# Moving gamma's load from ScalarE's queue to SyncE's, between and behind the halves of the first tile

## The chip, the cores and the metric

One core of a Trainium2 chip. The metric is the time of one execution on the device in microseconds (us). Before the change it was 239.57 us, the median of 3 runs (239.4 to 239.84). Smaller is better; a change within 2% either way counts as the same. All runs told here are fast runs with a granted clock of 1.000.

## The reference

```python
# x: (8, 512, 2048) float32, gamma: (2048,) float32; result (8, 1024, 2048) float32
x_rep = np.repeat(x, 2, axis=1)
rms = np.sqrt((x_rep ** 2).mean(axis=-1, keepdims=True) + 1e-6)
return (x_rep / rms * gamma[None, None, :]).astype(np.float32)
```

Every row of x is normalised, multiplied by gamma and written twice. Read once and written once that is 33.6 MB in and 67.1 MB out.

## The kernel before

The 4096 rows are eight tiles of 512 rows (128 partitions, four rows each). A tile has a buffer of 64 KB a partition, of which there are three. Loads fill the second half of a buffer; results fill it from the front, and the store writes the whole buffer out.

```python
def load(i, eng, parts=1):
    y = rows.tile([P, K * R, D], f32, name="y")      # K = 4, R = 2, D = 2048
    step = K // parts
    for k in range(0, K, step):
        at = K * (R - 1) + k
        eng.dma_start(out=y[:, at : at + step, :], in_=x_t[i, :, k : k + step, :])
    ys.append(y)
# ... square: Square with a sum and Sqrt on ScalarE; scale: reciprocal and
# scalar_tensor_tensor (x * rstd * gamma) on VectorE; repeat: copies on ScalarE and VectorE ...
ctx.enter_context(tc.manual_schedule())
load(0, nc.sync, parts=2)
gamma_b = singles.tile([P, D], f32, name="gamma_b")
cuts = [0, *range(D // 4, D + 1, D // 8)]            # one piece of 512 elements, six of 256
for c0, c1 in zip(cuts, cuts[1:]):
    nc.scalar.dma_start(out=gamma_b[0:1, c0:c1], in_=gamma[c0:c1].partition_broadcast(1))
nc.gpsimd.partition_broadcast(out_ap=gamma_b[:], in_ap=gamma_b[0:1, :])
eps_t = singles.tile([P, 1], f32, name="eps_t")
nc.vector.memset(eps_t, eps)
load(1, nc.sync)
load(2, nc.sync)
loads_after = {2: (3, 4, 5), 4: (6, 7)}
for i in range(ntiles):                              # 8
    compute(i)                                       # 4 x (square, scale), then repeat
    store(i, 0, K)
    for j in loads_after.get(i, ()):
        load(j, nc.sync)
```

## Time and profile before

| | before |
|---|---|
| median of 3 runs | 239.57 us |
| span of the profiled run | 237.9 us |
| packets of SyncE's queue (q1), share of sixteen DMA engines' time | 98.5% |
| ScalarE, VectorE busy | 42%, 41% |

What the change touches is the way gamma comes in, and two rows of the list of costliest groups show it. The columns are line, engine, operation, output and inputs, shapes, count; then busy time and mean ns of one; then the idle time of the engine just before them and what ended most of it.

```profile
L74 DVE SCALAR_TENSOR_TENSOR y<-y,rstd,gamma_b 128x2048 f32<-128x2048 f32 x32 | 75.3, 2352 | 4.1 <-POOL gamma_b L96 3.0
...
L96 POOL PARTITION_BROADCAST gamma_b<-gamma_b x1 | 2.3, 2294 | 12.2 <-DMA y<-in_x_dram 12.2
```

VectorE waits 3.0 us for the broadcast, and the broadcast waits 12.2 us. The name behind the arrow, a load of x, is a trap: the broadcast needs no part of x. The eight completion semaphores are shared in turn, one of gamma's pieces and the second half of tile 0 count on the same one, and the profile names whichever it finds there. That it was gamma is told by the chain of waits, which the prediction quotes.

### The profile page before, as it was taken

The numbers are of one execution on the slowest core, as the hardware profiler recorded it, in microseconds if no ns is written. First come the engines' busy times: TensorE is split into PE (matmuls) and PEld (weight loads), VectorE is DVE, ScalarE is ACT, GpSimd is POOL, SyncE is SP. The second block draws the span as 40 slices with busy tenths as digits, with TensorE's granted clock in tenths as the row PEclk, the third lists the DMA queues.
The fourth block names the chain that finished last, engine by engine and source line by source line (L and its number), as shares of the span: only waits on it lengthen the run. The fifth ranks groups of instructions, "written<-read, shape, count | busy, mean of one in ns | idle before, by whom it ended". The sixth has DMA issues, their size and how long they took to land.

```text
span 237.9 us, 287 instructions
## 1 busy us (share of the span) xinstructions
DVE 96.5 (41%) x73; ACT 101.0 (42%) x106; POOL 2.5 (1%) x5
## 2 busy tenths in 40 slices
DVE  0049999960000000059999960000199990000000
ACT  2697999900000000099999920000599960000000
POOL 0030000000000000000000000000000000000000
DMA  7999998989899998999998999989998989999994
GB/s 265 436 446 441 441 441 353 530 353 496 386 452 430 397 485 353 441 441 441 441 518 364 464 419 430 452 369 430 435 518 364 518 364 485 397 452 430 408 474 176
DMA packets 2464, 100.69 MB, mean 423 GB/s; under 512 B 279, under 2 KB 285, under 8 KB 286
## 3 DMA queue, kind: packets, MB, share of 16 engines
q1 hardware_dynamic: 2448, 100.66, 98.5%
q14 instruction: 2, 0.02, 0.0%
q10 hardware_dynamic: 14, 0.01, 0.0%
HBM read 33.56 MB, written 67.11 MB: 423 GB/s over the span
## 4 chain that ended last, share of the span: by engine, by line
DMA 58%; ACT 12%; DVE 9%; issue 1%; POOLq 1%; ACTq 1%; SPq 0%
DMA y<-in_x_dram 33%; DMA out_dram<-y 21%; ACT sq L64 8%; DVE y L74 7%; DMA gamma_b<-in_gamma_dram 4%; ACT y L81 3%; DVE y L81 2%; ACT rms L68 1%; POOLq L136 1%; ACTq L95 1%; DVE rstd L73 0%; POOLq L96 0%; SPq L56 0%
## 5 line engine op out<-in xcount | busy, mean ns | idle before, releaser
L64 ACT ACTIVATE sq<-y 128x2048 f32<-128x2048 f32 x32 | 59.7, 1865 | 87.8 <-DMA y<-in_x_dram 87.8
L74 DVE SCALAR_TENSOR_TENSOR y<-y,rstd,gamma_b 128x2048 f32<-128x2048 f32 x32 | 75.3, 2352 | 4.1 <-POOL gamma_b L96 3.0
L73 DVE RECIPROCAL rstd<-rms 128x1 f32<-128x1 f32 x32 | 5.0, 158 | 94.6 <-ACT rms L68 94.3
L81 ACT COPY y<-y 128x4096 f32<-128x4096 f32 x8 | 28.7, 3590 | 1.4 <-DVE y L74 1.4
L81 DVE COPY y<-y 128x4096 f32<-128x4096 f32 x8 | 18.3, 2294 | 0.3
L68 ACT ACTIVATE rms<-ss,eps_t 128x1 f32<-128x1 f32 x32 | 9.4, 295 | 1.0
L64 ACT ACTIVATION_READ_ACCUMULATOR sq<-y 128x1 f32 x32 | 6.0, 187 | 0.0
L64 ACT ACT_TABLE_LOAD x1 | 1.3, 1283 | 3.0 <-issue 3.0
L96 POOL PARTITION_BROADCAST gamma_b<-gamma_b x1 | 2.3, 2294 | 12.2 <-DMA y<-in_x_dram 12.2
L68 ACT ACT_TABLE_LOAD x1 | 1.3, 1283 | 0.0
L98 DVE MEMSET eps_t<- 128x1 f32 x1 | 0.1, 59 | 0.8 <-PEq L125 0.8
L125 POOL MEMSET const-uint8-127<- 128x1 uint8 x1 | 0.1, 102 | 0.0
L125 POOL MEMSET const-bfloat16-1.0<- 128x1 bf16 x1 | 0.1, 101 | 0.0
L125 POOL MEMSET const-float32-0.0<- 128x1 f32 x1 | 0.1, 98 | 0.2 <-issue 0.2
L125 POOL MEMSET const-float32-1.0<- 128x1 f32 x1 | 0.1, 98 | 0.0
## 6 DMA issues: line engine op xcount, KB each, us to landing
y<-in_x_dram SPq DMA_DIRECT2D x7, 4096.0 KB, 14.6
y<-in_x_dram SPq DMA_DIRECT2D x2, 2048.0 KB, 7.4
out_dram<-y SPq DMA_DIRECT2D x8, 24.4
gamma_b<-in_gamma_dram ACTq DMA_DIRECT2D x6, 1.0 KB
gamma_b<-in_gamma_dram ACTq DMA_DIRECT2D x1, 2.0 KB
```

Of the source, the lines that this page charges most:

```text
L64: nc.scalar.activation(out=sq[:], in_=ys[i][:, K * (R - 1) + k, :], func=Act.Square, accum_out=ss[:])
L68: nc.scalar.activation(out=rms[:], in_=ss[:], func=Act.Sqrt, scale=inv_d, bias=eps_t[:])
L73: nc.vector.reciprocal(out=rstd[:], in_=rms[:])
L74: nc.vector.scalar_tensor_tensor(out=ys[i][:, R * k, :], in0=ys[i][:, K * (R - 1) + k, :], scalar=rstd[:], in1=gamma_b[:], op0=Alu.mult, o ...
L81: copy(out=y_r[:, k0:k1, 1, :], in_=y_r[:, k0:k1, 0, :])
L95: nc.scalar.dma_start(out=gamma_b[0:1, c0:c1], in_=gamma[c0:c1].partition_broadcast(1))
L96: nc.gpsimd.partition_broadcast(out_ap=gamma_b[:], in_ap=gamma_b[0:1, :])
L98: nc.vector.memset(eps_t, eps)
L125: nc = _bacc.Bacc("TRN2", target_bir_lowering=False, num_devices=1)
L136: with _tile.TileContext(nc) as tc:
```

## The change

Its intent can be read from its order: gamma no longer takes turns with the loads from a second queue, but goes on the loads' own queue, six pieces right behind the first half of tile 0 and one behind the second half. ScalarE no longer issues DMAs.

```diff
-    load(0, nc.sync, parts=2)
     gamma_b = singles.tile([P, D], f32, name="gamma_b")
     cuts = [0, *range(D // 4, D + 1, D // 8)]
-    for c0, c1 in zip(cuts, cuts[1:]):
-        nc.scalar.dma_start(out=gamma_b[0:1, c0:c1], in_=gamma[c0:c1].partition_broadcast(1))
+
+    def gamma_piece(c0, c1):
+        nc.sync.dma_start(out=gamma_b[0:1, c0:c1], in_=gamma[c0:c1].partition_broadcast(1))
+
+    y0 = rows.tile([P, K * R, D], f32, name="y")
+    ys.append(y0)
+    load_half(y0, 0)                     # rows 0 and 1 of the tile, on SyncE
+    for c0, c1 in zip(cuts[:-2], cuts[1:-1]):
+        gamma_piece(c0, c1)
+    load_half(y0, 1)                     # rows 2 and 3
+    gamma_piece(cuts[-2], cuts[-1])
     nc.gpsimd.partition_broadcast(out_ap=gamma_b[:], in_ap=gamma_b[0:1, :])
```

The rest of the diff only splits the helper `load` into `load_half` and `load` and drops its engine argument.

## The prediction

> **What bounds the kernel now.** I read the engine totals first, then the slices, then the queues.
>
> ```profile
> DVE 96.5 (41%) x73; ACT 101.0 (42%) x106; POOL 2.5 (1%) x5
> ...
> DMA  7999998989899998999998999989998989999994
> ...
> q1 hardware_dynamic: 2448, 100.66, 98.5%
> q14 instruction: 2, 0.02, 0.0%
> q10 hardware_dynamic: 14, 0.01, 0.0%
> HBM read 33.56 MB, written 67.11 MB: 423 GB/s over the span
> ```
>
> VectorE and ScalarE work two fifths of a span of 237.9 us; the DMA engines are at 8 or 9 tenths in every slice but the first and the last. The queue table says what they do: q1 is the queue of SyncE, with all loads and stores, and its packets alone fill 98.5% of what sixteen engines could do in the span. q10 is ScalarE's queue, with fourteen packets: seven pieces of gamma, each a data packet and a 4-byte packet that counts the semaphore. So the time is a start before the first packet (1.6 us), 100.7 MB at full rate, and an end. 100.66 MB over the 235.2 us from the first q1 packet (at 1.73) to the last (236.77, both from the packet records of the trace) is 428 GB/s; nothing in the kernel can make that shorter except fewer bytes, and nothing makes it longer unless the queue runs dry. The whole question is therefore whether the change leaves the queue dry anywhere, or takes such a gap away.
>
> The place to look is the start, where the change is. The chain of waits tells how gamma sits there, and the timeline the consequences:
>
> ```profile
> 0.72 0.51 ACTq L95
> ...
> 2.69 9.71 DMA gamma_b<-in_gamma_dram
> ...
> 12.55 2.35 POOLq L136
> 14.90 0.02 issue
> 14.92 2.35 DVE y L74
> ...
> 24.69 2.30 DVE y L81
> ...
> 27.05 25.77 DMA out_dram<-y
> 52.84 48.32 DMA y<-in_x_dram
> ```
>
> ScalarE issues seven pieces; the last, issued at 2.69, lands 9.71 us later at 12.40. Then GpSimd spreads the row over the partitions (2.3 us), VectorE runs its first multiplication at 14.92 and is busy without a break until 26.99, and the store of tile 0 is issued at 27.05. The chain names gamma at its beginning, which makes it look as if earlier gamma were earlier everything. It is not so, and the next step shows why: the store takes 25.77 us to land, far more than its own 8.39 MB need (19.6 us at 428 GB/s), because it stands in the queue behind loads. The counting packets of the load of tile 2 come at 32.41 to 33.00 in the packet records: until then the DMA engines have loads to do, whatever VectorE does. From an issue to its first packet pass about 1.0 us (0.72 to 1.73 for the first load), so the store of tile 0 could be issued as late as about 31.4 without a gap. It is issued at 27.05: **4.3 us of slack**.
>
> SyncE's own waits show a coupling that the diff does not:
>
> ```profile
> SPq L52 <- DMA y<-in_x_dram: 5.7, 1, 5.7
> ...
> SPq L52 <- DMA gamma_b<-in_gamma_dram: 0.9, 1, 0.9
> ```
>
> The DMAs take eight completion semaphores in turn. The second half of tile 0 now shares the one of gamma's first piece and waits 0.9 us for it (issue at 2.03); the load of tile 1 shares that of the first half and waits 5.7 us (issue at 8.11).
>
> **What the Trainium skill says.** On "DMA: Bandwidth & Descriptors", section "Queues, rings and completion order": SyncE and ScalarE each own one row of rings on the same sixteen engines, an engine takes turns between rows at packet boundaries, and inside a ring descriptors are consumed in order. The trace agrees: the last four gamma pieces land at 8.57, 9.85, 11.12 and 12.40, 1.27 us apart, which is two 16 KB packets of the load (0.61 us each in the packet records) plus two tiny ones. Each of gamma's packets waited its turn behind one 16 KB packet. Section "Why a DMA increments its semaphore by 16 and not by 1" of the same page: a copy that can't be split runs on one engine, and the sequencer adds the rest of the count at once. The trace agrees: each gamma semaphore has one update 0.3 to 0.6 us after the issue and one more at landing, where a load has sixteen. Section "Issuing engines are not separate DMA queues": starting DMAs from several engines saves only sequencer time. That is what the change gives up, and I work it out below.
>
> **The change, part by part.** I read the order and the waits of the two builds. The work of VectorE, ScalarE, GpSimd and TensorE is the same, instruction for instruction, but for the seven DMA issues that leave ScalarE. SyncE now issues: first half, gamma 0 to 5, second half, gamma 6, tile 1, tile 2, then as before. The semaphores fall differently: the second half waits for nothing; gamma 6 waits for the first half to land; tile 1 waits for gamma 0, and tile 2 for gamma 1.
>
> 1. ScalarE loses seven issues, 2.23 us in the timeline (0.72 to 2.95). Its table load then runs some 2 us earlier, but its first square waits for the first half anyway (8.12). Worth 0.
>
> 2. Six issues stand before the second half on SyncE. On ScalarE the first piece took 0.51 us and the others came every 0.285 us: 0.54 + 5 x 0.285 = 2.0 us. The second half goes from 2.03 to about 0.72 + 0.38 + 2.0 = 3.1. The fastest engine ends the first half at 7.25 (its counting packet), so issue by 6.2 is early enough: 3.1 us of slack. Cost 0.
>
> 3. Gamma 0 to 5 stand behind the first half in the ring and no longer take turns with it. They start when the engine that carries them has done its eight packets, by about 7.6, and land at about 8.0 to 8.5, where now they come at 2.0 to 11.1.
>
> 4. Gamma 6 is the piece that decides, as the broadcast needs all seven. It waits for the first half (all sixteen counts at 8.10 now; the same after), is issued at 8.1 and gets behind the second half, which is in the ring already. Counting packets of the second half are at 12.11 to 12.62. Gamma 6 follows at about 12.6, and from a counting packet to the semaphore pass 0.4 us (12.01 to 12.40 for the last piece now): it lands at about 13.0 against 12.40. So gamma comes **0.6 us later**, not earlier: the first six gain, the seventh loses, and the seventh counts.
>
> 5. Broadcast, the first multiplication and the store of tile 0 shift by 0.6: 13.2, 15.5 and 27.65. This takes 0.6 from 4.3 us of slack. The store of tile 1 goes from 39.22 to 39.8 and that of tile 2 from 51.39 to 52.0; store 0 ends its packets at about 52, so both are still queued in time. The load of tile 3 waits for store 0 to land (52.82), which has not moved, and from there on everything is as before. Cost 0.
>
> 6. Tile 1 is issued after gamma 6, at 8.45 in place of 8.11; needed by 12.11 - 1.0 = 11.1. Cost 0.
>
> 7. The fourteen small packets run on one engine, now back to back: 98 ns for the 2 KB, 46 ns for each 1 KB, 9 ns for a counting packet, 0.44 us in sum, before and after. In the end the last packets of the engines lie at 235.4 to 236.8, so that engine has room. Cost 0.
>
> Sum: 239.57 + 0 = **239.6 us**.
>
> **The rivals.** (a) Gamma is on the path, as the chain says. Then 0.6 us later gives 240.2, or, if the author's intention holds and all of gamma lands near 8.5, up to 4 us earlier gives 236. The slices speak against both: no slice between 6 and 232 us falls to what an empty queue would look like (the lowest are 8 tenths, and in the bytes a low slice has a high neighbour, 353 beside 530), so there is no idle DMA time to buy back. (b) The small packets, back to back in one ring, stall it: if each counting packet held the ring until the write before it is confirmed, at the 0.4 us above, six pieces would put one engine 2.4 us behind, and as no engine ever idles, the lag would last to the end: 242 us, 1% slower. Against it: after every counting packet of a load the next 32 KB packet starts within 10 ns (21.793 and 21.799). For it: no ring has run such a row of tiny packets yet. I give this 5%. (c) SyncE becomes late: the second half misses the end of the first. It would take 3.1 us more of issue than I count, ten times the cost of a piece. (d) Fewer turns between two rows make the engines a little quicker in the first 12 us. The 16 KB packets take 0.61 us with turns and without (engines that carry no gamma show the same), so at most the 0.1 us by which first packets crowd.
>
> **Range and chances.** The three runs before span 0.44 us; I take that on each side, a little more upward for (b) and for another chip or hour: 239.0 to 240.3. A change by over 2% is 4.8 us; faster is impossible while the bytes stay, slower would need a stall twice that of (b).
>
> **What would show it.** In the profile after: q10 gone and q1 at 2462 packets, still about 98.5%; six gamma pieces landed before 9 us and the last at about 13; the broadcast at 13.2 where it is 12.60 now; store 0 issued at about 27.6 but landing at 52.8 as now; load 3 issued at 52.8. A broadcast before 12 would show step 4 wrong, but the time would still stand. Wrong altogether would I be if the GB/s of the first three slices fell by a tenth, or one engine's packets ran 1 us or more behind the others from 13 us to the end.

## The result, and the profile after

| | before | after |
|---|---|---|
| median, first comparison (6 runs each) | 239.59 us | 239.66 us |
| median, second comparison (11 and 6 runs) | 239.53 us | 239.70 us |
| ratio, first and second | | 1.0006 [0.9989, 1.0023], 1.0011 [0.9999, 1.0023] |
| span of the profiled run | 237.9 us | 237.8 us |

A ratio is the mean time of one kernel's fast runs over that of the other's of the same rounds, so not quite the ratio of the medians quoted. The change does nothing that can be told from noise; the second interval allows a loss of up to 0.23% (0.55 us) and practically no gain.

The page of the kernel after, in the parts that the prediction showed of before: the DMA row of the forty slices, the queues, and the two rows of groups.

```profile
DMA  7999998989999998999998999989998999999994
...
q1 hardware_dynamic: 2462, 100.67, 98.6%
q14 instruction: 3, 0.02, 0.0%
...
L76 DVE SCALAR_TENSOR_TENSOR y<-y,rstd,gamma_b 128x2048 f32<-128x2048 f32 x32 | 75.3, 2352 | 4.8 <-POOL gamma_b L107 3.7
...
L107 POOL PARTITION_BROADCAST gamma_b<-gamma_b x1 | 2.3, 2293 | 13.0 <-DMA gamma_b<-in_gamma_dram 13.0
```

q10 is gone and its fourteen packets are on q1. The engines are as full as before. VectorE's wait has grown from 3.0 to 3.7 us, and GpSimd's from 12.2 to 13.0 us: the broadcast of gamma starts 0.8 us later.

The issues of SyncE, from the timeline (start, length, both in us), and its own wait:

```profile
0.72 0.38 SPq L50 DMA_DIRECT2D y<-in_x_dram  x1
...
1.16 1.81 SPq L97 DMA_DIRECT2D gamma_b<-in_gamma_dram  x6
3.01 0.36 SPq L50 DMA_DIRECT2D y<-in_x_dram  x1
8.27 0.22 SPq L97 DMA_DIRECT2D gamma_b<-in_gamma_dram  x1
...
8.53 0.83 SPq L54 DMA_DIRECT2D y<-in_x_dram  x2
```

```profile
SPq L97 <- DMA y<-in_x_dram: 4.9, 1, 4.9
```

Six pieces cost 1.81 us of issue ahead of the second half. The seventh waits 4.9 us for the first half, because it is the ninth DMA and must have the first half's semaphore. The chain of waits shows what follows:

```profile
2.72 6.32 DMA gamma_b<-in_gamma_dram
...
9.11 4.25 issue
13.35 2.36 POOLq L147
15.71 0.03 issue
15.74 2.35 DVE y L76
...
25.50 2.30 DVE y L83
...
27.86 24.85 DMA out_dram<-y
52.72 0.02 issue
52.73 48.34 DMA y<-in_x_dram
```

The sixth piece has landed at 9.04. The 4.25 us of "issue" after it are a wait that the chain does not name: in the trace's semaphore records the seventh piece lands at 13.32. From there everything is later by 0.8 us, the broadcast (13.41), the first multiplication (15.74), the store of tile 0 (27.86), but the store lands at 52.72, 0.1 us sooner than before, and the load of tile 3 is issued at 52.73 where it was 52.84. The 0.8 us have vanished in the queue.

### The profile page after: what moved, and what is told of

Read it like the earlier page. It is cut to its first block, busy times and chain, and to the rows that moved or that the text cites. A ratio compares the mean times of both kernels' runs of the same rounds, so it can differ in the third digit from the quotient of the medians.

```text
span 237.8 us, 286 instructions
## 1 busy us (share of the span) xinstructions
DVE 96.5 (41%) x73; ACT 101.0 (42%) x106; POOL 2.5 (1%) x5
## 4 chain that ended last, share of the span: by engine, by line
DMA 56%; ACT 12%; DVE 9%; issue 3%; POOLq 1%; SPq 1%
DMA y<-in_x_dram 33%; DMA out_dram<-y 21%; ACT sq L66 8%; DVE y L76 7%; ACT y L83 3%; DMA gamma_b<-in_gamma_dram 3%; DVE y L83 2%; ACT rms L70 1%; POOLq L147 1%; SPq L97 1%; DVE rstd L75 0%; SPq L50 0%; POOLq L107 0%; SPq L58 0%
```

## The experiments

All are edits of the kernel after, all gave the right result, and all were timed in five rounds against the kernel before. For each I read from the packet records of the trace when the DMA engines were done with a transfer: the mean over sixteen engines of the 4-byte packet that follows it. All in us:

| kernel | store 0 issued | loads of tile 2 done | store 0 done | store 2 done | load of tile 5 done | last store done | time (median) |
|---|---|---|---|---|---|---|---|
| before | 27.05 | 32.68 | 52.03 | 90.67 | 119.75 | 235.87 | 239.57 |
| after | 27.86 | 32.62 | 51.94 | 90.58 | 119.70 | 235.90 | 239.66 |
| x3, gamma first | 24.03 | 32.70 | 52.02 | 90.65 | 119.74 | 235.82 | 239.72 |
| x6, one piece between | 24.06 | 32.67 | 51.99 | 90.63 | 119.73 | 235.83 | 239.63 |
| x9, 1 copy | 28.92 | 31.92 | 51.25 | 90.16 | 120.03 | 236.09 | 239.51 |
| x1, 2 copies | 30.18 | 31.62 | 50.94 | 90.01 | 120.09 | 236.11 | 239.85 |
| x8, 2 copies and 2 in tile 3 | 30.17 | 31.63 | 50.96 | 89.99 | 119.19 | 236.27 | 240.11 |
| x5, 4 copies | 32.85 | 31.76 | 53.16 | 92.71 | 122.80 | 238.93 | 242.60 |
| x2, 8 copies | 37.84 | 31.66 | 58.15 | 97.65 | 127.72 | 243.76 | 247.44 |
| x4, seven pieces between | 24.88 | 35.05 | 54.37 | 93.00 | 122.09 | 238.14 | 241.99 |

The theory: the queue of loads hides when gamma comes, as long as store 0 is issued before the rings are empty (a ring is the part of SyncE's queue that waits at one of the sixteen engines). The main rival: gamma is on the path, as the chain of waits has it. A turn is the place in the rings where loads end and stores begin, or the other way round; a packet is stretched when it takes longer than most of its size (1.213 us for 32 KB, 2.418 us for 64 KB).

### x1, x2, x5, x9: gamma made later, step by step

VectorE copies gamma onto itself 1, 2, 4 or 8 times after the broadcast, so that all that hangs on gamma comes later by about 1.26 us a copy (start to start; store 0 was issued 1.06, 2.32, 4.99 and 9.98 us later than in the kernel after), and nothing else changes. The memset of eps is put ahead of it, or the roots on ScalarE would wait too.

```diff
+    eps_t = singles.tile([P, 1], f32, name="eps_t")
+    nc.vector.memset(eps_t, eps)
     nc.gpsimd.partition_broadcast(out_ap=gamma_b[:], in_ap=gamma_b[0:1, :])
-    eps_t = singles.tile([P, 1], f32, name="eps_t")
-    nc.vector.memset(eps_t, eps)
+    for _ in range(2):                   # x9: 1, x5: 4, x2: 8
+        nc.vector.tensor_copy(out=gamma_b[:], in_=gamma_b[:])
```

x1, expected:

> Changed kernel plus 2 in-place copies of gamma on VectorE (128x2048, estimated 1.2 us each from 2.29 us for 128x4096) after the broadcast, so that everything up to the store of tile 0 comes 2.4 us later. Slack theory: store 0 is issued at 27.86 + 2.4 = 30.3, its packets come at 31.3 at the latest, before the load of tile 2 leaves the engines (32.1 to 33.0): no gap, time 239.6, ratio to the kernel before 1.000. Rival, gamma on the path: every us counts, 242.0, ratio 1.010.

Measured 239.85 us, ratio 1.0012 [1.0, 1.0025]. Store 0 was issued at 30.18, 3.1 us later than in the kernel before, and the rings did not run dry: each engine went from its last load packet to the first store packet within 10 ns.

x2, expected:

> The same with 8 copies, 9.6 us. Slack theory: store 0 is issued at 37.5, its packets start at 38.5, the engines have been dry since 32.6 on average: 5.9 us lost for good, 245.5, ratio 1.025, and the slice from 29.7 to 35.7 shows the gap. Rival, gamma on the path: 249.2, ratio 1.040. Rival, nothing at the start counts: 239.6.

Measured 247.44 us, ratio 1.0328 [1.0314, 1.0342]. The gap is there, in stretches of the timeline, first of the kernel after, then of this one. The columns are the stretch, its length, busy us of VectorE, ScalarE and GpSimd with counts, clock, share of the DMA engines, GB/s. A packet counts whole where it starts, so 0.86 in the kernel after is no gap.

```profile
33.00:36.00 3.00, 2.96 (x3) 3.00 (x2) 0.00 (x0) 1.00 0.86 371
```

```profile
27.00:33.00 6.00, 5.93 (x6) 2.45 (x1) 0.00 (x0) 1.00 0.62 268
33.00:36.00 3.00, 2.93 (x3) 3.00 (x3) 0.00 (x0) 1.00 0.00 0
36.00:40.00 4.00, 3.96 (x3) 3.94 (x6) 0.00 (x0) 1.00 0.61 262
```

No packet starts from 33 to 36 us, and none is under way. In the GB/s of the forty slices (6.1 us each) it is the sixth number:

```profile
GB/s 269 446 459 443 427 5 341 512 341 512 341 512 341 512 512 256 427 427 427 428 428 490 363 501 352 501 352 427 437 443 475 437 480 373 501 352 501 352 501 181
```

Each engine stood still for 7.1 us on average (31.66 to 38.74), and the kernel lost 7.9. The time alone decides nothing here: 247.4 lies about midway between my 245.5 and the rival's 249.2 (only the second rival, 239.6, is out). The gap decides, and the runs with shorter delays. I had expected a loss of 5.9, and where the miss lies is told by the table, against the kernel after. Store 0 was done 6.2 us later: the gap of 7.1, less 1.0 because the loads were done sooner (31.66, not 32.62). In the kernels before and after the last 32 KB load packet ahead of store 0 took 1.6 to 2.3 us on every engine, where the others take 1.213; with store 0 still far away it did not. Up to there the loss is near the 5.9 expected, but in part by luck: the gap was 1.2 longer than I wrote, and the stretch that fell away made up for 1.0 of it. Then 0.9 more were lost at the turn from store 2 to the loads (7.1 later) and another 0.9 at the turn from the load of tile 5 to store 3 (8.0 later), where packets were stretched that are not in the kernel after.

x5, expected:

> Changed kernel plus 4 in-place copies of gamma on VectorE, 1.26 us each as measured. Slack theory, with what the runs with 2 and 8 copies showed (store 0 issued at 30.18 and 37.84, first store packet 0.85 us after an issue into empty rings, loads done at 31.64 on average): store 0 is issued at 32.7, its packets come at 33.55, 1.9 us of empty rings: between 241.5 (the gap alone) and 242.4 (8 copies' loss less 4 copies). Rival, the loss grows evenly with the delay (0.98 us for each copy from the 8-copy run): 243.5. The 2-copy run (0.12% slower) already speaks against it.

Measured 242.60 us, ratio 1.0123 [1.0108, 1.0138], 0.2 above the upper edge of what I had written. The empty rings are 2.0 us here (31.76 to 33.7), the loss 3.0. The remaining 1.0 can be followed in the table against the kernel after: 1.2 at the end of store 0, 2.1 at the end of store 2, 3.1 at the end of the load of tile 5, and 3.0 at the end. The rival of an even loss, 243.5, is refuted. Again two later turns cost 0.9 and 1.0, and the first turn cost nothing where it had cost 0.9.

x9, expected:

> Changed kernel plus 1 copy: store 0 at about 28.9, 2.7 us before the loads end. Slack theory: no gap, 239.6 to 239.9. Lead theory of the turn: between the 4.1 us of the changed kernel (0.69 to 0.89 us stretched) and the 1.5 us of 2 copies (none), so it tells where the stretch begins; if there is none, the loads of tile 2 end near 31.6.

Measured 239.51 us, ratio 0.9995 [0.998, 1.001]. No gap and no loss. The last load packets were stretched by 0.21 us an engine on average, six of the sixteen.

The four together give the shape. With store 0 issued at 27.05, 27.86, 28.92 and 30.18 the ratios lie between 0.9995 and 1.0012; at 32.85 it is 3 us longer and at 37.84 almost 8. From 4 to 8 copies it rises by 4.84 us for 4.99 us of delay, nearly one for one. The rival, every us of lateness in full, would have given 2.5 us for two copies, and there were 0.3. The latest harmless issue lies between 30.18 and 32.85; an estimate is 30.6: the first engine done with the loads at 31.44 (in x1), less the 0.85 us that passed from an issue into empty rings to its first packet (37.84 to 38.69).

### x3 and x6: gamma made earlier

x3 loads gamma whole, as one piece of 8 KB, first of all on ScalarE's queue; x6 puts the same piece on SyncE's queue between the halves. In both there are so few DMAs at the start that none shares a semaphore, so tiles 1 and 2 are also issued at once; that is a second difference, which I did not part from the first, and it too should do nothing.

```diff
-    for c0, c1 in zip(cuts[:-2], cuts[1:-1]):
-        gamma_piece(c0, c1)
-    load_half(y0, 1)
-    gamma_piece(cuts[-2], cuts[-1])
+    # x3, ahead of the first half:
+    nc.scalar.dma_start(out=gamma_b[0:1, :], in_=gamma.partition_broadcast(1))
+    # x6, here:
+    nc.sync.dma_start(out=gamma_b[0:1, :], in_=gamma.partition_broadcast(1))
+    load_half(y0, 1)
```

x3, expected:

> Changed kernel, but gamma as one piece of 8 KB on ScalarE's queue, at the very start (only 4 loads and this piece, so no load waits for a shared semaphore either). Gamma lands near 2.5, the broadcast is done near 5, the first multiplication waits only for ScalarE, near 12, and VectorE's last copy is limited by the second half: store 0 near 24.5, 3 us earlier than in either kernel. Slack theory: time 239.6, ratio 1.000 (within 0.2%). Rival, gamma on the path: 236 to 237, ratio 0.987.

Measured 239.72 us, ratio 1.0007 [0.9994, 1.0019]. The broadcast began at 2.65, and store 0 was issued at 24.03, 3.8 us sooner than in the kernel after.

x6, expected:

> Changed kernel with gamma whole, as one piece of 8 KB between the halves: the change's order without its seventh piece and without any shared semaphore. Gamma lands near 8.3, the broadcast ends near 10.8, store 0 is issued near 24.0, 3.9 us earlier than in the changed kernel. Slack theory: the second half is issued near 1.6, no ring runs dry, 239.6, ratio within 0.2% of 1. Rival, gamma on the path: 236.

Measured 239.63 us, ratio 1.0008 [0.9996, 1.0019]. The chain of waits of x6 has gamma in it no more, and the same end of store 0:

```profile
0.72 7.29 DMA y<-in_x_dram
...
24.06 28.75 DMA out_dram<-y
...
52.82 48.36 DMA y<-in_x_dram
```

Store 0 was issued at 24.06, 3.8 us sooner than in the kernel after, and took 28.75 us to land where it took 24.85: it landed at 52.81 against 52.72. What is gained ahead of the queue is spent standing in it. This settles the rival: gamma as early as it can come is worth nothing here.

### x4: all seven pieces between the halves

One might ask why the change leaves the last piece behind the second half. This puts it ahead.

```diff
-    for c0, c1 in zip(cuts[:-2], cuts[1:-1]):
+    for c0, c1 in zip(cuts[:-1], cuts[1:]):
         gamma_piece(c0, c1)
     load_half(y0, 1)
-    gamma_piece(cuts[-2], cuts[-1])
```

> Changed kernel, but the seventh piece also ahead of the second half. The second half then is the ninth DMA and shares the semaphore of the first half: it can be issued only at 8.27, its packets come at 9.3, the engines are dry from 7.3 to 7.9 on. Gamma lands near 9.2, 4 us earlier than in the changed kernel; store 0 near 24.7. Slack theory: what counts is the dry queue, 1.8 us, not gamma: 241.4, ratio 1.0075. Rival, gamma on the path: 236 to 237.

Measured 241.99 us, ratio 1.0104 [1.0088, 1.0119]. Gamma was 4.3 us earlier (broadcast at 9.06 in place of 13.41) and the kernel 1% slower. SyncE's wait says why, and the stretch from 7 to 10 us, first of the kernel after and then of this one, what came of it:

```profile
SPq L50 <- DMA y<-in_x_dram: 4.3, 1, 4.3
```

```profile
7.00:10.00 3.00, 0.00 (x0) 1.73 (x1) 0.00 (x0) 1.00 1.00 428
```

```profile
7.00:10.00 3.00, 0.00 (x0) 2.09 (x3) 0.94 (x1) 1.00 0.44 101
```

The second half of tile 0, now the ninth DMA, waited 4.3 us for the semaphore of the first and was issued at 7.89, when that had landed, and the rings stood empty for 1.65 us on average. The first packets into the empty rings then took 0.6 us longer an engine, as they also do at the very start; together 2.25, and the end is 2.24 us later. I had expected 1.8 and left the second part out.

### x7: the change once more

The kernel after, unaltered, on the chip of x5 and x6.

> The changed kernel itself, unaltered, for a closer ratio on one chip beside the two others: 239.6, ratio 1.000 within 0.2%; a loss of 0.6 to 0.8 us, as if gamma's lateness counted, would be 1.0025 to 1.0033.

Measured 239.70 us against 239.53, ratio 1.0011 [0.9999, 1.0023]. A loss of 0.8 us (1.0033) is excluded, one of 0.1% is not, but x3 and x6, where gamma comes far earlier, stand at 1.0007 and 1.0008. So if that 0.1% is real, it also stands where gamma is not late.

### x8: is there a microsecond in the turns?

In x1 the loads of tile 2 were done 1 us sooner and it was lost later. If a turn from loads to stores is slow only when the store has waited long, then making store 3 late too should keep that gain, and the kernel would beat both.

```diff
 # x1, and in compute(i), after the four scales:
+        if i == 3:
+            for _ in range(2):
+                nc.vector.tensor_copy(out=gamma_b[:], in_=gamma_b[:])
```

> The 2-copy kernel plus 2 more in-place copies in tile 3, so that its store too is issued 2.5 us later. It asks about the turn from loads to stores: with 2 copies the last load packets ahead of store 0 were not stretched (loads of tile 2 done at 31.62 on average against 32.62 in the changed kernel), but those ahead of store 3 were (0.92 us an engine, store 3 issued at 115.12, 4.0 us before the loads would have ended). Theory, a turn is stretched only when the store has waited in the queue for some us: store 3 is now issued at 117.6, 1.5 us ahead, no stretch, 239.85 - 0.9 = 238.9, ratio 0.998 to the kernel before. Rival, the stretch is not set by that lead (store 5 waits 18 us ahead of its turn and stretches 0.04): no gain, 239.6 to 239.9.

Measured 240.11 us, ratio 1.0017 [1.0005, 1.0029]. At store 3 it was as the theory had it: the load of tile 5 done at 119.19, with no packet of that turn stretched, the best of all runs. But then the turn ahead of store 5, which had cost at most 0.18 us in the other runs, stretched by 0.80 us an engine with the same 18 us of waiting, and the end was 0.4 us later than in the kernel after. The theory that the wait sets the stretch falls. And the ratio's interval lies above 1: this run was some 0.2% slower than the kernel before with no empty ring. In the runs without a gap the stretches of 32 KB and 64 KB packets came to 1.1 to 1.6 us an engine in sum, and what moved was mostly their place. What sets the place I do not know; no run tells it.

## Why the prediction was right

It said 239.6 us in 239.0 to 240.3, and 239.66 and 239.70 came. By its steps:

**What bounds the kernel.** Right, and shown from both sides: the time answers to empty rings (x2, x4, x5) and not to gamma (x3, x6, x9, x1). Two slips: the 235.2 us from 1.73 to 236.77 are 235.0, and the rate stays 428 GB/s; and that nothing makes the kernel longer but a dry queue is too strong, as x8 lost some 0.2% (its interval is 0.05% to 0.29%) with its rings full.

**Steps 1 and 2, the issues.** Right in kind. ScalarE's table load moved ahead to 0.72 and its first square still waited for the first half, at 8.27. The second half was issued at 3.01 (3.1 predicted), and no ring ran dry. x4 shows what a late second half costs: issued at 7.89, it left the rings empty for 1.65 us.

**Step 3, six pieces back to back.** They landed at 8.10 to 9.04; predicted was 8.0 to 8.5. Their packets follow one another within 0.33 us (7.56 to 7.89), but the landings are 0.19 us apart. I had taken the spacing of the packets for that of the landings.

**Step 4, the seventh piece decides.** Right, and mis-sized: 13.32 where I wrote 13.0. Its packet ran at 12.75 and the counting packet behind it at 12.79, but the landing came 0.53 us later, not 0.4; and the engine that carried gamma was done with the second half at 12.74, 0.12 beyond the latest of before. The last of gamma landed 0.9 us later, not 0.6, and the broadcast began 0.8 later.

**Step 5, the slack.** The mechanism was right; the slack was mis-sized, and that it did not matter is because the change used so little of it. I took 4.3 us, from loads that end at 32.4 to 33.0. Those ends contain the 0.9 us by which the last load packets were stretched in these kernels, where store 0 had been queued for 3.8 us or more by the time the loads would have ended (in x1, 1.4 us ahead, none was). Without that the loads end at 31.44 to 31.9, and the latest harmless issue is by the estimate above 30.6: the slack was about 3.5 us, of which the change took 0.8. (In x5 and x2 the delay against the kernel before, less the empty time, is 3.8 and 3.7.) A change that made gamma later by 4.3 us I would have called free; by these numbers (an estimate) it would leave the rings empty for 0.6 us: 27.05 + 4.3 + 0.85 = 32.2 against 31.62 on average.

**Step 6, tile 1 later.** Issued at 8.53 (8.45 predicted), and harmless.

**Step 7 and rival (b), small packets in one ring.** No stall: an engine goes from each counting packet to the next data packet within 10 ns in this row too (the first, at 7.553, to 7.559; the next, at 7.639, to 7.645). The six pieces cost that engine 0.33 us of packets. Followed packet by packet to the end, it was done at 235.88 before and at 236.37 after, and the last of the sixteen at 236.77 and 236.62: it was not the last in either.

**Rival (a), gamma on the path.** Refuted by x3 and x6 in one direction and by x9 and x1 in the other. The chain of waits was no lie: gamma does release the store. But its next piece, a store that takes 24 to 29 us for 19.3 us of packets, told that the store stands in a line.

None of the signs of being wrong came: the first three slices moved 262, 439 and 447 GB/s (265, 436 and 446 before), and the last engine ended 0.7 us after the mean of the sixteen (0.9 before).

Open is a difference of 0.1% between the kernels, which neither comparison can tell from zero, and the cause of the stretched turns.

## What to carry to other kernels

When one queue keeps the DMA engines full, work out when it would first run dry, and compare each change only with that: here a wait before it cost nothing that could be told from noise, and after it every microsecond counted in full. Before reordering DMAs look at which completion semaphores they will share: one DMA too many ahead of a load (x4) cost 1%, and neither the diff nor the page of totals tells it, only the waits of the built program. And measure slack by adding a delay of known length until the time moves; what is read off the trace of the undisturbed kernel can hold a cost of its own.

## What the Trainium skill lacked or had wrong

- "DMA: Bandwidth & Descriptors", section "Where 436 GB/s comes from", says without a condition that between HBM and SBUF the HBM side, some 358 GB/s, binds. That does not hold for this program, which runs on one core: its loads and stores of 100.66 MB ran at 428 GB/s from first to last packet, near the 425 GB/s that the same page's table of measured loads has for one core (there 358 is the share when both cores of a pair stream). In steady state every 32 KB packet took 1.213 us and every 64 KB packet 2.418 us on its engine, which for sixteen engines is 432 and 434 GB/s.
- The same page, section "Anatomy of one DMA — SWDGE (gpsimd) path", gives a DMA on that path about 2 us of fixed cost. No section gives a figure for how much of a small DMA's cost on SyncE's path occupies the engine: six gamma pieces back to back took 0.33 us of one engine, and their landings followed 0.19 us apart.
- The same page has nothing on the turn from loads to stores in one ring: the last 32 KB load packet of each engine took 1.76 to 2.34 us ahead of store 0 in the kernel before, 1.213 in x1, and what was saved there (1.0 us) was lost again at later turns.
- No page says that where DMAs share a completion semaphore a profile can name the wrong one: the broadcast's wait of 12.2 us is put down to a load of x that it does not need.
